# Holding TensorE's written order in one group, moving a background reduction, and scaling the feed-forward input in another place

## The chip, the cores and the metric

The kernel runs on one core of one Trainium2 chip. The metric is the device time of one execution in microseconds (us). The core has a matrix engine (TensorE, in the profile PE for products and PEld for weight loads), a vector engine (VectorE, DVE), a scalar engine (ScalarE, ACT), GpSimd (POOL), and SyncE (SP), which here issues transfers only. Each engine works through its own queue in order.

## The reference

One layer of a bidirectional encoder block in 32-bit floats, with 256 tokens of width 2048, followed by a final RMS norm:

```python
mod = silu(c) @ ada_w + ada_b            # 12288 values: shift, scale, gate, twice
h = rms_norm(x, norm_mix_w) * (1 + scale_m) + shift_m
proj = h @ w_in                          # inputs of both branches, gates
y_a = (sigmoid(a_o) * rms_norm(mlstm_fwd + mlstm_bwd)) @ w_branch_a     # 4 heads
y_b = (rms_norm(delta_fwd + delta_bwd) * silu(b_z)) @ w_branch_b        # 16 heads
x = x + gate_m * ((g_a * y_a + g_b * y_b) @ w_out)
hf = rms_norm(x, norm_ffn_w) * (1 + scale_f) + shift_f
gt, up = split(hf @ w_gate_up)
x = x + gate_f * ((silu(gt) * up) @ w_down)
return rms_norm(x, norm_final_w)
```

The delta rule (branch B) needs, for each head, direction and chunk, the inverse of a unit triangular matrix. The kernel inverts 32 x 32 blocks on VectorE and puts larger ones together with small matrix products.

## The kernel before

**Products.** Every large product is made in three passes: a weight tile is split into a high part (`wh`, ScalarE, line 171 or 197) and a low part (`wl`, VectorE, line 172 or 198), and TensorE sums high x high, high x low and low x high. Weights arrive in pieces of 1 MB in four `raw` buffers (issued by SyncE); `wh` and `wl` have three buffers each. A product of 512 columns is a `tjob` of 8 steps with 12 matmuls each (k0 of two kinds per piece); a product of 128 columns is an `fjob` of 2 steps with 24 narrower matmuls.

**Filling jobs.** Around the delta rule, such jobs wait in the list `fills`: `v`, `mb`, `o`, `a`, `ma` (inputs of the mLSTM branch and the merge gates; in the trace the names raw_v, acc_ma and so on) and `z`. `fill(n)` issues their next n steps between the stages of other work. After every second step of a `tjob`, and once an `fjob`, `pump()` counts, and every `every[0]`-th count issues one *sum*.

**Sums.** The modulation values of parts 2 to 5 are not made on TensorE. Sum b of a part loads 1 MB of `ada_w` (transposed) and multiplies and adds it on VectorE (line 127): 16 sums and one small addition a part. Parts 2, 3 and 4 go into the list `background` before the delta rule (line 874), part 5 behind the product with `w_out` (line 1172). Beside the pumps, the loop of that product issues sums at listed steps (line 1163), and at step 4 of its last quarter all that are left.

**The delta rule.** Four groups of four heads (line 891). Per group: `invert` (VectorE, 30 dependent pairs of small products, lines 663 and 669, between filling steps; its result is stored to memory), `gdn_blocks` (loads it back, transposes it, mixes it into `R`, lines 682 to 689, and copies it to `X` and `UL`), and then two pairs of heads, each with stages in which TensorE, VectorE and ScalarE alternate: p1 (line 717, reads `R`), p2, p3, p4 (lines 726 to 751), pa, pb, pc (lines 763 to 776), po (785 to 790), px (796). Between two stages come one to four steps of the next group's head jobs `b` or of filling jobs; the tuple `last` (line 864) sets how many in the last group. As written, in that group: the end of o2 and all of a2, p1 of the first pair, ma2, mb3, o3 and the start of a3 spread over the stages, and behind the last stage the rest of a3, ma3, the first mLSTM products (`psc`, line 957), the rest of ma3 and `yb` (the product with `w_branch_b`).

**Who orders the work.** The program is traced in the written order and then scheduled by a planner that simulates it: on each engine, the first-written instruction that is ready in the simulation goes next. So a filling step can be moved ahead of a stage that isn't ready. `order(...)` pins an instruction behind everything traced before it on its engine, with no wait for its end. Before the change, TensorE's instructions of the delta rule are not pinned.

**The feed-forward input.** The product with `w_out` runs in quarters o0 to o3; o3 ends token half by token half. For each half, `residual` (lines 1113 to 1115) and `token_rstd` give the norm's factor `rs1`. Then `normed` scales x by quarters into `xn` (two buffers), `moved` transposes two halves on TensorE (`pxn`, line 1200), applies scale and shift (line 1204 or 1206) and takes the high part, and `low` the low part. This is pinned, and interleaved with the steps of the first gate job `gt0`: step n of `gt0` uses blocks 2n and 2n+1.

Of the kernel before, what the change touches and what calls it, by code (L numbers as in the profile page):

```python
# [12 lines left out]
ALU = mybir.AluOpType  # L13
# [38 lines left out]
@with_exitstack  # L52
def hybrid_block(ctx: ExitStack, tc: tile.TileContext, xr, nfr, crow, pk_d, cst_d, ada2, ada4, win0, winb, wint, wba, wbb, wo, wgu, wd, out, dbg=None):
    nc = tc.nc
    V, S, G, PE = nc.vector, nc.scalar, nc.gpsimd, nc.tensor

    def pool(stack, name, bufs=1, **kw):
        return stack.enter_context(tc.tile_pool(name=name, bufs=bufs, **kw))
# [27 lines left out]
    def order(ins, yes=True):  # L86

        return tc.keep_in_program_order(ins) if yes else ins
# [46 lines left out]
    def row_store(part, rp, factor=1.0):  # L135

        pr = gps(f"row{part}")
        PE.transpose(pr[0:KB, 0:P], mod[:, part * KB : (part + 1) * KB], ident)
        sm = rp.tile([KB, P], F32, name=f"rowsm{part}")
        S.activation(sm, pr[0:KB, 0:P], AF.Copy, scale=factor)  # L140
        G.dma_start(row_d[part].rearrange("(b p) -> b p", b=KB), sm)
# [5 lines left out]
    count, every = [0], [0]  # L147

    def sums(n=1):

        while n and background:
            if next(background[0], None):
                n -= 1
            else:
                background.pop(0)
# [89 lines left out]
    def run(job):  # L245
        for _ in job:
            pass
# [3 lines left out]
    def fill(n=1):  # L251

        while n and fills:
            if next(fills[0], None):
                n -= 1
            else:
                fills.pop(0)
# [85 lines left out]
    def z_job(g, early=0):  # L343
        def done(ps):
            szs[g] = evp.tile([P, 2, 512], F32, tag="sz", bufs=1, name=f"sz{g}")
            for t in range(2):
                S.activation(szs[g][:, t], ps[t], AF.Silu)
        return tjob(f"z{g}", [wint[g, u] for u in range(4)], hh, hl, done, early)
# [329 lines left out]
    def gdn_blocks(g):  # L678

        cg = bk.tile([P, 2, 512], F32, tag="uu", bufs=1, name=f"cg{g}")  # L680
        for b in range(4):
            G.dma_start(cg[32 * b : 32 * b + 32, 0], inv_d[g][:, 16 * b : 16 * b + 16].rearrange("j m i -> j (m i)"))
        yield
        order(V.transpose(cg[:, 1], cg[:, 0]))
        F_, Bt, Ft, B_ = (cg[:, i // 2, (i % 2) * 256 : (i % 2 + 1) * 256].rearrange("p (m c) -> p m c", m=8) for i in range(4))

        def mix(dst, a, ca, b, cb):
            order(V.tensor_scalar(dst, b, cb, None, ALU.mult))
            order(V.scalar_tensor_tensor(dst, a, ca, dst, ALU.mult, ALU.add))

        mix(R[:, 0], Ft, even, Bt, odd)
        mix(R[:, 1], B_, even, F_, odd)
        yield
        for i, ab in enumerate(((Ft, Bt), (B_, F_))):
            for b in range(4):
                r = slice(32 * b, 32 * b + 32)
                order(S.activation(X[r, i, :, b % 2], ab[b // 2][r], AF.Copy))
            yield
        for i, a in enumerate((F_, B_)):
            for b in range(4):  # L700
                r = slice(32 * b, 32 * b + 32)
                order(S.activation(UL[r, i, :, r], a[r], AF.Copy))
            yield
# [132 lines left out]
    def stream(h0):  # L836

        todo = []

        def piece():  # L840

            for q in list(todo):
                q[0] -= 1
                if not q[0]:
                    todo.remove(q)
                    next(heads1[q[1]])

        for h in range(h0, min(h0 + 2, NH_B)):
            for j in range(3):
                for _ in b_job(h, j):  # L850
                    piece()
                    yield True
            todo += [[2, h], [4, h]]
        while todo:
            fill(1)
            piece()
            yield True
        while True:
            fill(1)
            yield True  # L860
# [16 lines left out]
    def invert(g):  # L877
        gen = gdn_invert(g)
        next(gen)
        fill(4)  # L880
        for _ in gen:
            fill(1)

    def o_load(g, where, bufs):
        o4 = where.tile([P, 4, T], F32, tag="o4", bufs=bufs, name=f"o4_{g}")
        G.dma_start(o4, ob_d[g].rearrange("h p t -> p h t"))
        return o4
# [3 lines left out]
    for g in range(4):  # L891
        if g == 3:
            sf.close()
            op = pool(so, "op", side="right")
        blocks = gdn_blocks(g)
        next(blocks)
        fill(8)
        next(blocks)
        fill(1)
        pairs = [gdn_phase2(g, p) for p in range(2)]  # L900
        every[0] = (0, 2, 2, 2)[g]
        for p in range(2):
            pieces = stream(4 * g + 2 * p + 4)
            if g == 3:
                o4s += [o_load(i, op, 3) for i in ((0, 1), (2,))[p]]
            for n in range(1, 10):
                next(pairs[p], None)
                if p == 0:
                    next(blocks, None)
                for _ in range(after[n] if g < 3 else last[n]):  # L910
                    next(pieces)
            for _ in pairs[p]:
                pass

            if g < 3:
                while 4 * g + 2 * p + 5 not in heads:
                    next(pieces)
        if g < 3:
            fills.insert(0, z_job(g + 1))
            every[0] = 0  # L920
            invert(g + 1)
# [146 lines left out]
    fill(4)  # L1068
    next(cores)
    fill(1000)  # L1070
    so.close()
    sa.close()
    sd = ExitStack()
# [14 lines left out]
    mgh, mgl = big(bigC, F32R, "mgh"), big(bigC, F32R, "mgl")  # L1088
    for g in range(4):
        if g == 3:  # L1090
            every[0] = 0
            while len(background) > 2:
                sums()
            row_store(2, ml, 0.5)
        run(y_a(g, mgh, mgl))
# [21 lines left out]
    def root():  # L1117

        order(S.activation(rs1[:, 2:3], ones1, AF.Sqrt))
# [8 lines left out]
    rs1 = xp.tile([P, 3], F32, name="rs1")  # L1128
# [23 lines left out]
    for g in range(4):  # L1152
        def done_o(*a, g=g):
            for t, ps in [a] if g == 3 else enumerate(a[0]):
                residual(t, g, ps, gm, ss1, wp, g == 3)
                if g == 3:
                    token_rstd(ss1, rs1, t)

        if g == 3:
            root()  # L1160
        between = (lambda: next(gt0)) if g == 3 else None
        for i, _ in enumerate(tjob(f"o{g}", [wo[g, u] for u in range(4)], mgh, mgl, done_o, by_token=between)):
            if i in ((4, 6, 7), (1, 2, 4, 6), (1, 2, 4, 6), (1, 2, 4))[g]:
                sums()
            if g == 3 and i == 4:
                sums(P)
                V.scalar_tensor_tensor(
                    affn, mod[:, 4 * KB : 5 * KB], 1.0, pk[:, PK_NFFN : PK_NFFN + KB], ALU.add, ALU.mult
                )
# [16 lines left out]
    def normed(q, t, parts, eng):  # L1186
        if q not in xns:
            xns[q] = hp.tile([P, 2, 512], F32, tag="sg", bufs=2, name=f"xn{q}")
        o, i = xns[q][:, t, parts], x1[:, t, q * 512 + parts.start : q * 512 + parts.stop]
        if eng is V:  # L1190
            order(V.tensor_scalar(o, i, rs1[:, t : t + 1], None, ALU.mult))
        else:
            order(S.activation(o, i, AF.Copy, scale=rs1[:, t : t + 1]))

    def moved(b):

        px = gps(f"pxn{b}")
        for t in range(2):
            f = b % 4 * P
            order(PE.transpose(px[:, t * P : (t + 1) * P], xns[b // 4][:, t, f : f + P], ident))  # L1200
        hfs[b] = hp.tile([P, T], F32, tag="hf", bufs=2, name=f"hf{b}")
        f, m = affn[:, b : b + 1], mod[:, 3 * KB + b : 3 * KB + b + 1]
        if b % 2 and b > 2:
            order(S.activation(hfs[b], px[:, 0:T], AF.Identity, scale=f, bias=m))
        else:
            order(V.tensor_scalar(hfs[b], px[:, 0:T], f, m, ALU.mult, ALU.add))
        order(S.activation(hfh[:, b], hfs[b], AF.Copy))
# [5 lines left out]
    normed(0, 1, slice(0, 256), V)  # L1213
    for t in range(2):
        normed(0, t, slice(256, 512), S)
    moved(0)
    moved(1)
    low(0)
# [4 lines left out]
    for b in range(2, KB, 2):  # L1223

        next(gt0)
        low(b)
        low(b + 1)
        next(gt0)
        if b % 4 == 2 and b < 12:
            for t in range(2):  # L1230
                normed(b // 4 + 1, t, slice(0, 512), S)
        for e in (b + 2, b + 3):
            if e < KB:
                moved(e)
# [3 lines left out]
    for j in range(FB // 4):  # L1238
# [4 lines left out]
        for e2 in range(2):  # L1243
# [5 lines left out]
            b = 4 * j + 2 * e2  # L1249
# [144 lines left out]
```

## Time and profile before

| | |
|---|---|
| median of 3 runs | 1985.31 us (1982.88 to 1988.02) |
| the profiled execution | 1979.27 us, span 1977.3 us, mean granted clock of TensorE 0.988 |
| TensorE busy | 1918.9 us, 97% of the span |
| VectorE, ScalarE, GpSimd busy | 71%, 52%, 5% |
| memory traffic | 246 GB/s on average |
| one sum on VectorE | 2.29 us, 64 of them |

The stages in the trace, from the span's start: first product up to 138 us; delta rule's groups from about 314, 482, 665 and 862 us (their first p1); `yb` from 952, `ya` from 1076, o0 to o3 from 1169 to 1254, feed-forward input from 1260 to 1292, gate and up products to 1738, down product to the end.

A row of waits names the waiting instruction and, behind the arrow, who released it. In a row of a group stand the line, engine, operation, output and inputs, shapes and count, then busy us, mean ns of one, and the idle time of the engine before it. Durations of one execution are compared with its own span; the runs' median is another number.

### The profile page before, as it was taken

The numbers are of one execution on the slowest core, as the hardware profiler recorded it, in microseconds if no ns is written. First come the engines' busy times: TensorE is split into PE (matmuls) and PEld (weight loads), VectorE is DVE, ScalarE is ACT, GpSimd is POOL, SyncE is SP. The second block draws the span as 40 slices with busy tenths as digits, with TensorE's granted clock in tenths as the row PEclk, the third lists the DMA queues.
The fourth block names the chain that finished last, engine by engine and source line by source line (L and its number), as shares of the span: only waits on it lengthen the run. The fifth ranks groups of instructions, "written<-read, shape, count | busy, mean of one in ns | idle before, by whom it ended". The sixth has DMA issues, their size and how long they took to land.

```text
span 1977.3 us, 27036 instructions
## 1 busy us (share of the span) xinstructions
PE 1918.9 (97%) x10352; PEld 1705.5 (86%) x10352; DVE 1402.5 (71%) x2091; ACT 1022.7 (52%) x1568; POOL 96.9 (5%) x185
## 2 busy tenths in 40 slices
PE   8999999999999999999799999799999999999997
PEld 6887889989989998998688888688888888888886
DVE  5779887878988996965587769766666655555554
ACT  3146657855765686465454444554444444444443
POOL 0000300110100011000200000000000000000000
PEclk9999999999999999999799999899999999999999
DMA  9996665567667765885677679466766765566563
GB/s 400 420 383 194 222 223 192 167 203 283 228 199 247 281 214 191 310 303 190 234 291 266 249 288 419 182 234 235 265 244 237 262 246 193 205 240 203 202 206 114
DMA packets 78675, 487.76 MB, mean 247 GB/s; under 512 B 10265, under 2 KB 15681, under 8 KB 23889
## 3 DMA queue, kind: packets, MB, share of 16 engines
q1 hardware_dynamic: 63360, 450.95, 62.2%
q0 software_dynamic: 7872, 19.99, 4.4%
q10 hardware_dynamic: 7314, 15.10, 2.1%
q8 instruction: 81, 1.33, 0.3%
q14 instruction: 48, 0.39, 0.1%
HBM read 469.16 MB, written 16.83 MB: 246 GB/s over the span
## 4 chain that ended last, share of the span: by engine, by line
PE 73%; DVE 11%; DMA 9%; ACT 4%; issue 2%; POOL 0%; SPq 0%; ACTq 0%; DVEq 0%; POOLq 0%
DMA ra<-ada 5%; PE acc_up L215 4%; PE acc_up L218 4%; PE acc_up L216 4%; PE acc_d L216 4%; PE acc_d L215 4%; PE acc_d L218 4%; PE acc_gt L216 4%; PE acc_gt L215 4%; PE acc_gt L218 4%; PE acc_o L218 2%; PE acc_o L216 2%; PE acc_o L215 2%; PE acc_a L175 2%; PE acc_b L175 2%
## 5 line engine op out<-in xcount | busy, mean ns | idle before, releaser
L198 DVE TENSOR_TENSOR wl_d<-raw_d,wh_d 128x1024 fp32r<-128x1024 f32 x88 | 107.8, 1225 | 102.7 <-ACT wh_d L197 102.7
L127 DVE SCALAR_TENSOR_TENSOR ada<-ada,crow 128x2048 f32<-128x2048 f32 x64 | 146.5, 2289 | 43.6 <-DMA ada<-ada 43.5
L198 DVE TENSOR_TENSOR wl_up<-raw_up,wh_up 128x1024 fp32r<-128x1024 f32 x88 | 107.5, 1225 | 95.9 <-ACT wh_up L197 95.9
L197 ACT ACTIVATE wh_d<-raw_d 128x1024 fp32r<-128x1024 f32 x88 | 93.0, 1057 | 130.5 <-PE acc_d L216 125.3
L198 DVE TENSOR_TENSOR wl_gt<-raw_gt,wh_gt 128x1024 fp32r<-128x1024 f32 x88 | 107.7, 1224 | 72.4 <-ACT wh_gt L197 68.2
L197 ACT ACTIVATE wh_gt<-raw_gt 128x1024 fp32r<-128x1024 f32 x88 | 92.9, 1056 | 120.7 <-PE acc_gt L216 73.2
L197 ACT ACTIVATE wh_up<-raw_up 128x1024 fp32r<-128x1024 f32 x88 | 93.0, 1056 | 118.2 <-PE acc_up L216 71.7
L215 PE MATMUL acc_gt<-wh_gt,hfh 128*128 128x512 f32 x352 | 135.2, 384 | 0.0
L216 PE MATMUL acc_gt<-wh_gt,hfl 128*128 128x512 f32 x352 | 134.6, 382 | 0.0
L175 PE MATMUL acc_b<-hh,wh_b 128*128 128x256 f32 x576 | 134.6, 276 | 0.0
L175 PE MATMUL acc_b<-hl,wh_b 128*128 128x256 f32 x576 | 134.6, 277 | 0.0
L215 PE MATMUL acc_up<-wh_up,hfh 128*128 128x512 f32 x352 | 133.5, 379 | 0.0
L216 PE MATMUL acc_up<-wh_up,hfl 128*128 128x512 f32 x352 | 133.5, 379 | 0.0
L216 PE MATMUL acc_d<-wh_d,ffl 128*128 128x512 f32 x344 | 130.4, 379 | 0.0
L215 PE MATMUL acc_d<-wh_d,ffh 128*128 128x512 f32 x344 | 130.4, 379 | 0.0
L530 PE MATMUL first<-x,raw 128*128 128x256 f32 x512 | 114.5, 382 | 7.5 <-ACT x L523 6.8
L530 PEld LDWEIGHTS first<-x,raw 128*128 128x128 f32 x512 | 96.1, 190 | 25.9 <-ACT x L523 12.4
L175 PEld LDWEIGHTS acc_b<-hl,wh_b 128*128 128x128 f32 x576 | 110.6, 192 | 0.4
L175 PEld LDWEIGHTS acc_b<-hh,wh_b 128*128 128x128 f32 x576 | 110.5, 192 | 0.5
L197 ACT ACTIVATE wh_o<-raw_o 128x1024 fp32r<-128x1024 f32 x64 | 67.1, 1054 | 58.9 <-PE acc_o L216 35.5
L218 PE MATMUL acc_gt<-wl_gt,hfh 128*128 128x512 f32 x352 | 95.3, 385 | 0.0
L171 ACT ACTIVATE wh_b<-raw_b 128x1024 fp32r<-128x1024 f32 x72 | 76.1, 1058 | 37.1 <-PE acc_b L175 22.8
(384 smaller groups left out, 5018.4 us busy)
## 6 DMA issues: line engine op xcount, KB each, us to landing
ada<-ada SPq DMA_DIRECT2D x64, 1024.0 KB, 5.8
raw_gt<-wgu SPq DMA_DIRECT2D x44, 1024.0 KB, 5.0
raw_up<-wgu SPq DMA_DIRECT2D x44, 1024.0 KB, 4.9
raw_d<-wd SPq DMA_DIRECT2D x44, 1024.0 KB, 4.9
raw_b<-winb SPq DMA_DIRECT2D x36, 1024.0 KB, 5.0
ra<-ada SPq DMA_DIRECT2D x32, 1025.0 KB, 15.8
raw<-win SPq DMA_DIRECT2D x16, 1024.0 KB, 17.1
raw_z<-wint SPq DMA_DIRECT2D x16, 1024.0 KB, 5.2
```

Source lines behind the costliest of these rows:

```text
L127: V.scalar_tensor_tensor(raw, raw, 1.0, row_c[:, :D], ALU.mult, ALU.mult, accum_out=mod[:, c0 + b : c0 + b + 1])
L171: S.activation(wh, raw[:, k0 : k0 + 8], AF.Copy)
L175: PE.matmul(o, wh[:, k], both(x, k0 + k).rearrange("p a b -> p b a"), start=k0 + k + i == 0, stop=False)
L197: order(S.activation(wh, raws[u][:, k0 : k0 + 2], AF.Copy), hold)
L198: order(V.tensor_tensor(wl, raws[u][:, k0 : k0 + 2], wh.bitcast(F32), ALU.subtract), hold)
L215: order(PE.matmul(ps[t], tok(xh, kk, t), turns(wh[:, k]), start=kk == 0, stop=False), early and steps > 1)
L216: PE.matmul(ps[t], tok(xl, kk, t), turns(wh[:, k]), start=False, stop=False)
L218: PE.matmul(ps[t], tok(xh, kk, t), turns(wl[:, k]), start=False, stop=kk == last)
L530: PE.matmul(first[o], raw[:, o], x[:, b], start=b == 0 and o % 2 == 0, stop=b == KB - 1 and o % 2 == 1)
```

## The change

TensorE's products and transposes go through a small class that pins them while `pin[0]` is true: from the start of the delta rule's last group to the end of the filling jobs. Group 0 of the delta rule issues a sum at every third count; `every[0] = 0` ahead of the last quarter of `ya` is gone, so it stays 2 until the feed-forward loop is over; the listed sums in o1 to o3 are fewer. `normed` can run on GpSimd, does so for quarter 1 early, and quarters 2 and 3 are scaled at blocks 4 and 8 and not at 6 and 10.

```diff
-    V, S, G, PE = nc.vector, nc.scalar, nc.gpsimd, nc.tensor
+    V, S, G = nc.vector, nc.scalar, nc.gpsimd
+    pin = [False]
+    class Tensor:
+        def matmul(self, *a, **k):
+            return order(nc.tensor.matmul(*a, **k), pin[0])
+        def transpose(self, *a, **k):
+            return order(nc.tensor.transpose(*a, **k), pin[0])
+    PE = Tensor()
...
         if g == 3:
             sf.close()
             op = pool(so, "op", side="right")
+            pin[0] = True
...
-        every[0] = (0, 2, 2, 2)[g]
+        every[0] = (3, 2, 2, 2)[g]
...
     fill(1000)
+    pin[0] = False
     so.close()
...
         if g == 3:
-            every[0] = 0
             while len(background) > 2:
                 sums()
...
-            if i in ((4, 6, 7), (1, 2, 4, 6), (1, 2, 4, 6), (1, 2, 4))[g]:
+            if i in ((4, 6, 7), (2, 4, 6), (1, 3), ())[g]:
                 sums()
...
-        if eng is V:
-            order(V.tensor_scalar(o, i, rs1[:, t : t + 1], None, ALU.mult))
+        if eng is not S:
+            order(eng.tensor_scalar(o, i, rs1[:, t : t + 1], None, ALU.mult))
...
+    for t in range(2):
+        normed(1, t, slice(0, 512), G)
     moved(0)
...
-        if b % 4 == 2 and b < 12:
+        if b % 4 == 0 and b < 12:
             for t in range(2):
                 normed(b // 4 + 1, t, slice(0, 512), S)
```

## The prediction

> **What bounds the kernel now.** I read the page first, then TensorE's waits, then stretches of the span, then single places. The profiled execution took 1979.27 us (span 1977.3 us, 2.0 us around it); the three runs have a median of 1985.31 us, 6.0 us above it. So I make the sum against 1979.27 us and add its difference to 1985.31 us. Repeated runs spread by 0.26%, so I take 0.3%, 6.0 us, as the least change that a measurement can tell from none.
>
> ```profile
> PE 1918.9 (97%) x10352; PEld 1705.5 (86%) x10352; DVE 1402.5 (71%) x2091; ACT 1022.7 (52%) x1568; POOL 96.9 (5%) x185
> ```
>
> TensorE sets the end; other engines count only where TensorE idles or its clock is low. TensorE's waits, over the whole span and then between 930 and 975 us, say where it idles (us in total, times, longest):
>
> ```profile
> PE pxn L1200 <- ACT xn L1193: 11.6, 7, 6.8
> ...
> PE psc L957 <- DMA mkq<-kq_d: 3.7, 2, 3.3
> PE acc_yb L215 <- ACT obh L932: 3.5, 1, 3.5
> PE px L796 <- DVE on L819: 3.3, 1, 3.3
> PE pb L775 <- DVE r L776: 2.3, 1, 2.3
> PE po L786 <- ACT z L768: 0.7, 1, 0.7
> ...
> PE pden L981 <- DVE mdec L966: 0.5, 1, 0.5
> ```
>
> Two places matter: the end of the delta rule's last group (3.7 + 3.5 + 3.3 + 2.3 + 0.7 + 0.6 + 0.5 = 14.6 us) and the feed-forward's input (11.6 us). Both also lower the clock. The stretches (length; busy us of PE, PEld, DVE, ACT, POOL; granted clock; DMA share; GB/s), and below them four short ones with PE alone:
>
> ```profile
> 336.00:420.00 84.00, 82.69 (x613) 78.63 (x614) 68.62 (x170) 64.71 (x142) 13.91 (x28) 1.00 0.55 159
> 817.00:861.50 44.50, 44.50 (x208) 38.99 (x207) 37.35 (x58) 20.68 (x25) 2.85 (x5) 1.00 0.85 312
> 930.00:982.00 52.00, 37.38 (x160) 30.70 (x159) 24.21 (x46) 23.50 (x43) 10.77 (x18) 0.77 0.60 212
> 1169.00:1253.00 84.00, 83.49 (x391) 72.91 (x390) 73.08 (x73) 36.87 (x46) 0.55 (x1) 1.00 0.98 400
> 945.90:956.30 10.40, 5.91 (x14) 0.51 0.47 158
> 966.40:980.20 13.80, 13.31 (x44) 0.51 0.47 158
> 1256.50:1263.50 7.00, 2.99 (x11) 0.51 0.00 0
> 1277.00:1280.50 3.50, 3.50 (x10) 0.51 0.00 0
> ```
>
> At half clock, half of the busy time is lost: (5.91 + 13.31) / 2 = 9.6 us at the group's end, 1.5 and 1.75 us at the feed-forward's input. So the group's end costs 14.6 + 9.6 = 24.2 us today, the feed-forward's input 11.6 + 3.25 = 14.9 us.
>
> **Part 1: TensorE's order held from the last group on.** The end is dry because the planner spent the filling jobs early. As written, the group's first product (p1, line 717) stands right behind job a2, and ma2, mb3 and the first sixth of o3 come only behind it. Where the trace has them:
>
> ```profile
> L177 PE MATMUL acc_a<-hh,wl_a x64: 275/275/276, 796.9 to 816.5; 128*128 128x256 f32 x64
> L717 PE MATMUL p<-R,cc x8: 192/276/276, 861.7 to 862.4; 128*128 128x32 f32 x8
> ```
>
> Held, TensorE comes to p1 at 816.8 us and not at 861.7 us; 44.9 us of fill (the 44.5 us full stretch above) stand queued behind it, and ScalarE and VectorE can split only three steps ahead. p1 reads R, the end of a chain: 60 small VectorE products of the inversion, a store, a load, a transpose, the mix. VectorE and its rows between 816 and 862 us, then the chain's end (start, length):
>
> ```profile
> L127 DVE SCALAR_TENSOR_TENSOR ada<-ada,crow 128x2048 f32<-128x2048 f32 x5 | 11.4, 2288 | 1.5 <-DMA ada<-ada 1.5
> L198 DVE TENSOR_TENSOR wl_mb<-raw_mb,wh_mb 128x1024 fp32r<-128x1024 f32 x8 | 9.7, 1217 | 1.4 <-ACT wh_mb L197 1.3
> L198 DVE TENSOR_TENSOR wl_ma<-raw_ma,wh_ma 128x1024 fp32r<-128x1024 f32 x6 | 7.3, 1214 | 0.2 <-ACT wh_ma L197 0.2
> L663 DVE TENSOR_TENSOR utmp<-uu 64x238 f32<-64x238 f32 (+13 forms) x14 | 4.4, 314 | 0.3
> L669 DVE TENSOR_TENSOR uu<-uu,utmp 64x238 f32<-64x238 f32 (+13 forms) x14 | 4.4, 313 | 0.2
> ```
> ```profile
> 844.05 0.17 DVE L669 TENSOR_TENSOR uu<-uu,utmp 64x30 f32<-64x30 f32 x1
> ...
> 857.03 0.71 DVE L684 STREAM_TRANSPOSE cg<-cg 128x512 f32<-128x512 f32 x1 [2.54 <-DMA cg<-inv_d]
> 857.67 0.31 DVE L688 TENSOR_SCALAR R<-cg,cst 128x256 f32<-128x256 f32 x1
> ...
> 859.03 0.48 DVE L689 SCALAR_TENSOR_TENSOR R<-cg,cst,R 128x256 f32<-128x256 f32 x1
> ```
>
> So R is far from ready at 816.8 us. But the chain will run faster: at that time 4.4 + 4.4 = 8.8 us of it are left, and what slows it today is the splitting of weights (9.7 + 7.3 us) and the modulation sums (11.4 us), which feed a TensorE that would now stand still. One more split and one sum remain: 816.8 + 8.8 + 1.2 + 2.3 = 829.1 us. Store and load took 857.03 - 844.22 = 12.8 us amid a DMA share of 0.85; I take 10.5, as the weight stream stops too (it keeps four raw buffers). Transpose and first mix: 0.71 + 0.31 + 0.48 = 1.5 us. R at 841 us: **a wait of 24 us**, bounded by 19 (only the 8.8 us and a 9 us transfer) and 43 (R at 859.5 us as now). Then some 4 us at half clock, as behind the stalls above: +2.0 us.
>
> What it buys. The waits that have to be covered, and how long psc was in coming:
>
> ```profile
> 946.25 0.73 PE L796 MATMUL px<-cst,on 128*128 128x128 f32 x2 [3.34 <-DVE on L819]
> 947.54 0.69 PE L796 MATMUL px<-cst,on 128*128 128x128 f32 x2 [0.56 <-ACT obt L798]
> ...
> 965.24 2.62 PE L957 MATMUL psc<-mkq 128*128 128x256 f32 x8 [3.33 <-DMA mkq<-kq_d]
> ```
>
> As written, behind every stage of the group stand one to three steps of a filling job (the full stretch above: 44.5 us / 208 = 0.214 us a matmul, 12 in a step, 2.6 us). Behind its last stage come 6 steps of a3 (24 narrow matmuls; the 192 of a2 in the first fence of this part took 21 us, so 2.7 us each), 4 of ma3, psc, 4 more of ma3, yb: 27 us before psc and 37 us before yb, where psc's data came 17 us behind px. I expect 3.5 us of the 24.2 to stay (z and r are waited for one step later): -20.7 us. Bounds: 0 and -24.2. **Part 1: +24 + 2 - 20.7 = +5.3 us.**
>
> **Part 2: the sums.** Counting the pumps of the filling jobs: group 0 has 16 (numbers 27 to 42), so every third gives 6 sums, where it had none. Groups 1 to 3, yb and ya0 to ya2 keep their 8, 8, 7, 8 and 6; ya3 gets 2. All 48 sums of three parts are then done by the first step of o1, where today 13 fall between 1169 and 1261 us:
>
> ```profile
> L127 DVE SCALAR_TENSOR_TENSOR ada<-ada,crow 128x2048 f32<-128x2048 f32 x13 | 29.7, 2287 | 2.6 <-DMA ada<-ada 2.6
> ```
>
> Cost: 6 x 2.29 = 13.7 us of VectorE put where it is busy 68.62 of 84 us. TensorE has fills there to run ahead with, so it will hardly stall at once; but the chain to R starts later, and what had been absorbed by more fill is, with part 1, added to the wait at p1. Bounds 0 and +13.7; I take **+4 us**, nearer to nothing, since VectorE had 15 us of idle time there. In o itself TensorE was busy 83.49 of 84 us, so the empty VectorE gains nothing before the last quarter's end.
>
> There it does (start, length):
>
> ```profile
> 1251.16 0.69 DVE L1113 TENSOR_TENSOR tmss<-acc_o,gm 128x512 f32<-128x512 f32 x1 [1.14 <-PE acc_o L241]
> 1251.77 2.28 DVE L127 SCALAR_TENSOR_TENSOR ada<-ada,crow 128x2048 f32<-128x2048 f32 x1
> ...
> 1256.05 0.67 DVE L1113 TENSOR_TENSOR tmss<-acc_o,gm 128x512 f32<-128x512 f32 x1
> ...
> 1257.37 2.28 DVE L127 SCALAR_TENSOR_TENSOR ada<-ada,crow 128x2048 f32<-128x2048 f32 x1
> ...
> 1258.02 0.19 ACT L1115 ACTIVATION_READ_ACCUMULATOR tmss<-x 128x1 f32 x1
> ...
> 1260.51 1.97 PE L1200 MATMUL pxn<-cst,xn 128*128 128x128 f32 x8 [6.79 <-ACT xn L1193]
> ```
>
> TensorE was done at 1260.51 - 6.79 = 1253.72 us. Without the two sums the second half's tm starts at 1253.75, 2.3 us sooner, and its reduce follows the square (1258.21) and not the sum (1259.65), 1.2 us more when the reads are counted: -3.5 us. But line 1091 also goes: every stays 2 until the loop of the feed-forward input is over, so two of gt0's four pumps (numbers 178 and 180) now put a sum of part 5 and its 1 MB load into that loop (the first takes a raw buffer ahead of gt0's last piece, on SyncE's queue). VectorE's held instructions behind the first (low(8)) queue behind it, and the planner can put it into the very gap that the old sums leave: +1 us (0 to +2.3).
>
> **Part 3: the scaling.** Today ScalarE scales a quarter directly ahead of its transposes; a row of the second such stop:
>
> ```profile
> 1275.75 0.33 PE L1200 MATMUL pxn<-cst,xn 128*128 128x128 f32 x1 [1.72 <-ACT xn L1193]
> ```
>
> The later stops together are 11.6 - 6.8 = 4.8 us, and the 1.75 us at half clock from 1277 us follow from this one. Quarter 1 goes to GpSimd, quarters 2 and 3 one turn (two blocks) ahead of use, and the buffers are free by then. GpSimd has no such row; its nearest is a memset of that shape, the ScalarE row is the same work:
>
> ```profile
> L552 POOL MEMSET cc<- 128x512 f32 x6 | 2.9, 521 | 5.7 <-DMA raw_v<-wint 5.7
> L1193 ACT ACTIVATE xn<-x,rs 128x512 f32<-128x512 f32 x6 | 4.0, 706 | 0.0
> ```
>
> Between 0.5 and, four times that, 2.1 us each (an estimate; I take 1.0, near the ScalarE row). The eight transposes and twelve matmuls ahead of quarter 1's give some 4.6 us, so even two of 2.1 us are hidden. I take 0.5 us of the stops as left: -4.3 - 1.75 = -6.0 us (bounds -2 and -6.6). **Parts 2 and 3: +4 - 3.5 + 1 - 6.0 = -4.5 us.**
>
> The wait ahead of the first transposes shrinks to 6.79 - 3.5 = 3.3 us. The 3.34 us stall before px lowered the clock, and the stop of 1.72 us did too, so I leave the 1.5 us of half clock there. The Trainium skill ("TensorE: Matmul & The Clock Gate", Part 1) has the clock halved only after an idle window of about 3.4 us; by it the clock would hold and the sum be 1.5 us lower. These rows speak against that.
>
> **Sum:** +5.3 - 4.5 = +0.8 us: 1980 us of the profiled kind, 1986 us as a median.
>
> **Rivals.** (a) *The wait at p1 is short, faster.* For: 11.4 + 9.7 + 7.3 = 28.4 of VectorE's 37.35 us between 817 and 861.5 us are sums and splits. Against: 12.8 us of transfers don't shrink with VectorE. With a wait of 10 us: 14 us less, 1972 us. (b) *The wait at p1 is as long as today's lead, slower.* The inversion keeps its pace, because the six sums of group 0 reach it late and other VectorE work stays planned between its steps; R comes at 860 us, the wait is 43 us: +19 us, 2005 us. It decides from a wait of 30 us on. For: 60 dependent steps and two transfers, all unhidden then. Against: the splits are held back by three buffers. (c) *The held order changes nothing*, as the planner's had been this one: then -4.5, and 3 of the sums' 4 us absorbed too, 1978 us. Against: p1 stands 44.9 us behind its written place.
>
> **Chances.** Forecast (within 6 us) 0.37; (a) 0.27; (b) 0.30; (c) 0.06. So faster 0.33, same 0.37, slower 0.30. Around the likeliest 1980 to 1992; the range reaches well into (a) and just short of all of (b): 1968 to 2004.
>
> **What would show it.** A TensorE wait of 20 us or more for R at line 717, no more waits at pb, px, yb and psc, clock 1.00 between 930 and 980 us; xn waits down to one of some 3.5 us; six sums between 310 and 420 us. The forecast is wrong if line 717 waits under 15 or over 30 us, or if the group's end stays dry.

## The result, and the profile after

The changed kernel takes 2055.42 us (median of 4 runs, 2049.6 to 2062.11), beside 1986.66 us for the kernel before in the same session: a ratio of 1.0349 (95% interval 1.0312 to 1.0387), 69 us slower. The forecast was 1986 us, with a range of 1968 to 2004. The profiled execution took 2049.6 us (span 2047.6). That of before (1979.27 us) lies some 7 us below its median, so spans of single executions differ by a little more than medians do; below, times are compared by ratios of runs, and the traces tell where they went.

From the page of the kernel after: TensorE's line, and TensorE and its granted clock in 40 slices of 51 us.

```profile
PE 1932.9 (94%) x10352; PEld 1712.3 (84%) x10352; DVE 1401.6 (68%) x2091; ACT 1027.5 (50%) x1569; POOL 100.5 (5%) x187
...
PE   8999999999998999459999999989999999999998
...
PEclk9999999999998999679999999999999999999999
```

TensorE does the same 10352 instructions and is 14 us busier, by lower clock; the rest of the 70 us of span is idle time. Most of both lies in the delta rule's end: from group 2's first product to `yb` TensorE idles 63 us (761 to 1031 us), in the kernel before 12 us (665 to 952 us). Waits of TensorE from 800 to 1050 us (us in total, times, longest; the matmuls now carry the line of the new class, so the tiles tell them apart), and stretches around the longest (length; busy us of PE, PEld, DVE, ACT, POOL; clock; DMA share; GB/s):

```profile
PE p L62 <- ACT X L709: 38.9, 1, 38.9
PE p L62 <- DVE pt L730: 5.5, 1, 5.5
PE pb L62 <- DVE r L788: 5.0, 2, 2.6
PE acc_ma L62 <- ACT wh_ma L209: 3.9, 1, 3.9
```
```profile
820.00:848.00 28.00, 20.75 (x100) 18.17 (x100) 13.75 (x52) 12.44 (x42) 3.94 (x8) 0.68 0.18 65
848.50:887.50 39.00, 0.48 (x3) 0.51 (x3) 23.03 (x73) 4.48 (x15) 8.65 (x14) 0.50 0.22 62
...
892.00:980.00 88.00, 81.26 (x445) 72.49 (x445) 45.97 (x56) 50.26 (x98) 0.00 (x0) 0.98 0.62 218
```

TensorE stands 38.9 us before the last group's first product, and the 28 us ahead of it are thin as well (20.75 us busy, at a clock of 0.68: the end of group 2's second pair, without fill between its stages). The old dry end is no longer dry: 81.26 of 88 us at a clock of 0.98.

What went wrong began far earlier. VectorE during the inversion ahead of group 1, from its first to its last instruction, in the kernel before (424.6 to 464.5 us: 40 us) and after (456.9 to 550.7 us: 94 us); columns: line, engine, operation, tiles and shapes, count, then busy us, mean ns of one, idle time before:

```profile
L198 DVE TENSOR_TENSOR wl_mb<-raw_mb,wh_mb 128x1024 fp32r<-128x1024 f32 x8 | 9.7, 1209 | 0.0
L663 DVE TENSOR_TENSOR utmp<-uu 64x58 f32<-64x58 f32 (+14 forms) x29 | 9.5, 326 | 0.8
L669 DVE TENSOR_TENSOR uu<-uu,utmp 64x58 f32<-64x58 f32 (+14 forms) x29 | 9.4, 325 | 0.7
L198 DVE TENSOR_TENSOR wl_ma<-raw_ma,wh_ma 128x1024 fp32r<-128x1024 f32 x4 | 4.8, 1210 | 0.0
L172 DVE TENSOR_TENSOR wl_b<-raw_b,wh_b 128x1024 fp32r<-128x1024 f32 x3 | 3.6, 1213 | 0.1
```
```profile
L184 DVE TENSOR_TENSOR wl_b<-raw_b,wh_b 128x1024 fp32r<-128x1024 f32 x24 | 29.0, 1210 | 0.2 <-ACT wh_b L183 0.2
L330 DVE SCALAR_TENSOR_TENSOR cv<-pad,pk,cv 128x256 f32<-128x256 f32 x40 | 18.2, 469 | 0.0
L139 DVE SCALAR_TENSOR_TENSOR ada<-ada,crow 128x2048 f32<-128x2048 f32 x8 | 18.2, 2280 | 1.9 <-DMA ada<-ada 1.9
...
L681 DVE TENSOR_TENSOR uu<-uu,utmp 64x30 f32<-64x30 f32 (+14 forms) x30 | 9.5, 318 | 0.4
L675 DVE TENSOR_TENSOR utmp<-uu 64x30 f32<-64x30 f32 (+14 forms) x30 | 9.5, 317 | 0.3
```

The inversion's own work is 19 us in both. In the kernel before it shares VectorE with the splits of filling jobs (`wl_mb`, `wl_ma`). In the kernel after the inversion starts 32 us later, but these filling jobs do not: `mb` runs from 440 to 464 us, in the kernel before from 438 to 459 us, so its splits are over when the inversion starts. TensorE works mostly on the next group's head jobs then: 24 splits, 40 convolution steps and 8 sums of group 1, 65 us, stand between the inversion's steps, beside 11 splits of filling jobs (`o`, `a`, `z`), 13 us. A head job brings VectorE two splits, four convolution steps and, every second time, a sum: 2 x 1.21 + 4 x 0.47 + 1.14 = 5.4 us, against the 5.4 us that TensorE takes for its two steps (2.7 us each, from the prediction's row of a2). By this estimate it fills VectorE by itself, while a filling step brings 1.21 us of split per 2.6 us. In the trace VectorE is busy 90.47 of the 93.5 us from 457 to 550.5 us, and TensorE all of them.

The feed-forward's input after: TensorE's waits, then rows of VectorE (start, length) and of GpSimd.

```profile
PE pxn L65 <- ACT xn L1206: 6.2, 1, 6.2
PE acc_gt L62 <- ACT hfh L1220: 4.0, 4, 2.7
```
```profile
1324.63 2.29 DVE L139 SCALAR_TENSOR_TENSOR ada<-ada,crow 128x2048 f32<-128x2048 f32 x1 [0.53 <-DMA ada<-ada]
...
1326.85 0.69 DVE L1127 TENSOR_TENSOR x<-x,tmss 128x512 f32<-128x512 f32 x1
...
1342.44 2.29 DVE L139 SCALAR_TENSOR_TENSOR ada<-ada,crow 128x2048 f32<-128x2048 f32 x1 [0.70 <-DMA ada<-ada]
```
```profile
1329.18 1.57 POOL L1204 TENSOR_SCALAR xn<-x,rs 128x512 f32<-128x512 f32 x1 [82.90 <-DVE rs L1138]
1331.97 1.73 POOL L1204 TENSOR_SCALAR xn<-x,rs 128x512 f32<-128x512 f32 x1 [1.22 <-DVE rs L1138]
```

The later `xn` stops are gone. The first sum of part 5 stands exactly in the gap that the old sums left, between the last product with the gate and the addition to x; the second delays `low` in the loop (the 2.7 us stop).

### The profile page after: what moved, and what is told of

The parts are those of the page before. It is cut to its first block, busy times and chain, and to the rows that moved or that the text cites. A ratio compares the mean times of both kernels' runs of the same rounds, so it can differ in the third digit from the quotient of the medians.

```text
span 2047.6 us, 27053 instructions
## 1 busy us (share of the span) xinstructions
PE 1932.9 (94%) x10352; PEld 1712.3 (84%) x10352; DVE 1401.6 (68%) x2091; ACT 1027.5 (50%) x1569; POOL 100.5 (5%) x187
## 5 line engine op out<-in xcount | busy, mean ns | idle before, releaser
L183 ACT ACTIVATE wh_b<-raw_b 128x1024 fp32r<-128x1024 f32 x72 | 76.2, 1060 | 64.5 <-PE acc_b L62 37.1
L210 DVE TENSOR_TENSOR wl_o<-raw_o,wh_o 128x1024 fp32r<-128x1024 f32 x64 | 77.2, 1219 | 31.8 <-ACT wh_o L209 31.5
```

Of the source, the lines that this page charges most:

```text
L183: S.activation(wh, raw[:, k0 : k0 + 8], AF.Copy)
L210: order(V.tensor_tensor(wl, raws[u][:, k0 : k0 + 2], wh.bitcast(F32), ALU.subtract), hold)
```

## The experiments

Differences in us are (ratio - 1) x the median of before in the same session (1983 to 1987 us).

### The change taken apart

`pin_alone` has only the hold, `group0_sums_alone` only `every[0]` of 3 in group 0, `scaling_alone` only the sooner scaling; `no_pin` is the change without the hold:

```diff
-            pin[0] = True
```

> The kernel before with TensorE's order held from the last group's start to the end of the filling jobs, and nothing else. Theory A (the hold and the six sums of group 0 cost so much only together: the sums let the filling jobs be spent early and make R late, the hold then forbids what is left to run): the wait at p1 is about the 24 us of the prediction's first part, the group's dry end is gone, and the time is 0 to 12 us above before. Theory B (the hold alone is the cause): 45 to 75 us above before, with a wait of 35 us or more at p1. Theory C (the sums of group 0 alone): within 6 us of before.

> The changed kernel without the hold (sums and scaling stay). Theory A: the late R is then partly covered by ma2, mb3 and o3, so 10 to 35 us above before. Theory B: 3 to 10 us below before. Theory C: 50 to 75 us above before, as much as the change itself.

> The kernel before with one edit: every third count of group 0 issues a sum (six sums more there, six fewer later). Theory A: 15 to 35 us above before, and the last group's first p1 at least 20 us later than the 862 us of before. Theory B: within 6 us. Theory C: 50 us or more above before.

> The kernel before with the third part alone: quarter 1 scaled on GpSimd early, quarters 2 and 3 at blocks 4 and 8. All theories: the stops of 1.5, 1.7 and 0.7 us ahead of the later transposes go, and with them the half clock after the second; 4 to 7 us below before if nothing takes their place, within 2 us of before if the steps of the first gate job become bound by VectorE or ScalarE instead (the changed kernel shows four waits for hfh, one of them 2.7 us beside a sum of part 5, three of 0.4 us without one).

| | ratio to before (95%) | us |
|---|---|---|
| hold alone | 1.0058 (1.0038 to 1.0078) | +11.5 |
| change without hold | 1.0306 (1.0274 to 1.0337) | +60.8 |
| group 0's sums alone | 1.0282 (1.0262 to 1.0302) | +56.0 |
| scaling alone | 0.9969 (0.9954 to 0.9983) | -6.2 |

The six sums are the fault, without the hold as with it. I had held a cost that only both together bring (theory A) for possible; it is refuted. Theory C, the sums alone, has all but one reading: it put the hold alone within 6 us of before, and that cost 11.5 us. In the run with these sums alone the inversion ahead of group 1 again takes 94 us (458.8 to 552.6), that ahead of group 2 takes 75 us, and the first products of groups 1, 2 and 3 come at 570, 763 and 956 us, where they came at 483, 665 and 862. TensorE stays busy meanwhile (it idles 11 us from 338 to 763 us); the bill comes where no fill is left. Stretches of before, then of this run:

```profile
800.00:955.00 155.00, 144.54 (x901) 131.82 (x901) 101.72 (x144) 81.85 (x140) 7.32 (x12) 0.97 0.72 256
955.00:1060.00 105.00, 100.84 (x456) 87.31 (x455) 78.66 (x115) 48.81 (x65) 8.75 (x16) 0.91 0.76 280
```
```profile
800.00:955.00 155.00, 139.13 (x821) 125.17 (x819) 113.77 (x221) 85.39 (x146) 17.25 (x31) 0.96 0.74 259
955.00:1060.00 105.00, 77.87 (x309) 66.39 (x310) 39.77 (x75) 42.75 (x100) 11.84 (x20) 0.64 0.33 109
```

Between 955 and 1060 us TensorE idles for 27 us and works the other 78 at a mean clock of 0.64: the last group's stages follow each other with no filling job between them (the last one, `ma`, ends at 946 us).

### Work, loads or order

The six sums in group 0 again, with VectorE's work on them taken away and their loads kept, so this version leaves these six values out (theory O is the order on VectorE, W the work, L the loads):

```diff
+            n = 2 if part == 2 and b < 6 else D
-            V.scalar_tensor_tensor(raw, raw, 1.0, row_c[:, :D], ALU.mult, ALU.mult, accum_out=mod[:, c0 + b : c0 + b + 1])
+            V.scalar_tensor_tensor(raw[:, :n], raw[:, :n], 1.0, row_c[:, :n], ALU.mult, ALU.mult, accum_out=mod[:, c0 + b : c0 + b + 1])
```

> The kernel before with the six sums in group 0, of which VectorE multiplies 2 columns in place of 2048 (the loads and the raw buffers stay; the sums of part 2's first six rows are left out, some 13.7 us of VectorE). Theory O (order): the cost of +56 us comes from where the planner puts the head jobs' splits and convolutions on VectorE, in between the steps of the inversions, since the inversion then starts after the next heads' jobs are already ready; it takes little to tip that, so this stays slower than before by 25 to 60 us, with the inversion of group 1 or 2 longer than 70 us. Theory W (work): the 13.7 us of VectorE in a stretch where it is full are multiplied along the chain; with the work gone the time is within 6 us of before and each inversion lasts about 40 us. Theory L (loads): the loads hold raw buffers and delay the weights behind them; also +25 or more, but with inversions of 40 us and TensorE waiting for wh.

Ratio 1.0171 (1.0155 to 1.0188), +33.9 us: without 13.7 us of VectorE work three fifths of the loss remain. The inversions ahead of groups 1 and 2 take 69 and 86 us, and in the second (636 to 722 us) VectorE does the work of the next head jobs again:

```profile
L173 DVE TENSOR_TENSOR wl_b<-raw_b,wh_b 128x1024 fp32r<-128x1024 f32 x23 | 27.8, 1210 | 0.0
L319 DVE SCALAR_TENSOR_TENSOR cv<-pad,pk,cv 128x256 f32<-128x256 f32 x40 | 18.3, 470 | 0.0
```

So W falls as the whole cause; the 22 us that went with the work may be its own price or a better order, which this run does not tell apart. L, which asked for inversions of 40 us, falls as the loads' direct cost; that the loads are what sets the inversion back (it starts at 438 and not 425 us) stands.

Then the head jobs' splits were kept behind the inversions, first all of them:

```diff
-            V.tensor_tensor(wl, raw[:, k0 : k0 + 8], wh.bitcast(F32), ALU.subtract)
+            order(V.tensor_tensor(wl, raw[:, k0 : k0 + 8], wh.bitcast(F32), ALU.subtract), name[0] == "b")
```

> The kernel before with the six sums in group 0 in full, and the low-part splits of the head jobs (b jobs, line 172) kept in program order on VectorE, so that none can stand between the steps of an inversion written ahead of it. Theory O: inversions back at about 40 us, cost against its control (the held splits alone) 5 to 16 us, the six sums' own 13.7 us of VectorE or less. Theory W: still 40 us or more above the control. Theory L: as W, with inversions of 40 us.

> The control: the kernel before with only the head jobs' splits kept in program order. All theories: 0 to +15 us (a held split can make TensorE wait for it in the groups' pairs, where products of the pairs and head jobs alternate), inversions about 40 us.

The control alone cost 1.0523 (1.0500 to 1.0546), +104 us and not the 0 to 15 expected: held splits make TensorE wait, 22 us at the groups' first products and 15 us in 8 waits at `vps` among others. With the six sums it is 1.0469 (1.0447 to 1.0491). The sums cost nothing there (it is even faster with them), and inversions take 34 to 42 us, but a kernel with this much idle time is a poor witness. So only the first split behind two inversions was held, with the mixes of `gdn_blocks` unpinned so that the split need not wait for them:

```diff
-            V.tensor_tensor(wl, raw[:, k0 : k0 + 8], wh.bitcast(F32), ALU.subtract)
+            order(V.tensor_tensor(wl, raw[:, k0 : k0 + 8], wh.bitcast(F32), ALU.subtract), name in ("b8_0", "b12_0") and k0 == 0)
...
-        order(V.transpose(cg[:, 1], cg[:, 0]))
+        V.transpose(cg[:, 1], cg[:, 0])
...
-            order(V.tensor_scalar(dst, b, cb, None, ALU.mult))
-            order(V.scalar_tensor_tensor(dst, a, ca, dst, ALU.mult, ALU.add))
+            V.tensor_scalar(dst, b, cb, None, ALU.mult)
+            V.scalar_tensor_tensor(dst, a, ca, dst, ALU.mult, ALU.add)
```

> The kernel before with the six sums in group 0, and of the head jobs' splits only the first one behind the inversions of groups 1 and 2 (b8_0 and b12_0, one instruction each) kept behind the inversion on VectorE; the mixes behind the inversion are left free. Theory O (the late inversion shares VectorE with the head jobs): the inversion of group 1 takes 20 to 30 us in place of 94 and that of group 2 about 40, the first product of group 1 comes at 505 to 525 us in place of 570, TensorE waits there 10 to 25 us as the fill work is used up, and the cost against its control is 10 to 30 us, in place of 56. Theory W (the sums' 13.7 us of VectorE or their loads do it wherever the head jobs stand): the cost against the control stays at 45 us or more.

> The control: the kernel before with only these two splits held and the mixes free. All theories: 0 to +25 us (the head jobs start up to 19 us later than the 464 us of before, some of it without other work for TensorE); inversions of 30 to 40 us.

Control 1.0129 (1.0099 to 1.0158), with the sums 1.0218 (1.0183 to 1.0252): the six sums cost 43.2 - 25.6 = 17.6 us (some 9 to 26), not 56. The inversion ahead of group 1 takes 26 us (459.1 to 485.1), and this time VectorE does little beside it:

```profile
L669 DVE TENSOR_TENSOR uu<-uu,utmp 64x30 f32<-64x30 f32 (+14 forms) x30 | 9.7, 323 | 1.0
L663 DVE TENSOR_TENSOR utmp<-uu 64x30 f32<-64x30 f32 (+14 forms) x30 | 9.7, 322 | 1.0
L198 DVE TENSOR_TENSOR wl_o<-raw_o,wh_o 128x1024 fp32r<-128x1024 f32 x2 | 2.5, 1226 | 0.2 <-ACT wh_o L197 0.2
L127 DVE SCALAR_TENSOR_TENSOR ada<-ada,crow 128x2048 f32<-128x2048 f32 x1 | 2.3, 2285 | 0.0
```

It starts 34 us late all the same, as in `group0_sums_alone`, and TensorE waits 20.1 us at group 1's first product, where it waits 12.0 us in the control and not at all in the kernel before (waits from 455 to 700 us):

```profile
PE p L717 <- DVE R L689: 25.0, 2, 20.1
```

So about two thirds of the 56 us hang on what stands between the inversion's steps. The share is rough, since part of the sums' cost can hide in the control's own 25.6 us of loss.

### Number or place

Three sums (every sixth job), three sums in the second pair alone, and six sums under the inversion itself:

```diff
-        every[0] = (0, 2, 2, 2)[g]
+        every[0] = (6, 2, 2, 2)[g]
```
```diff
             pieces = stream(4 * g + 2 * p + 4)
+            if g == 0:
+                every[0] = 3 * p
```
```diff
-        for _ in gen:
+        for i, _ in enumerate(gen):
             fill(1)
+            if g == 1 and i < 6:
+                sums()
```

> The kernel before with a sum at every sixth head job of group 0 in place of every third: three sums, not six. By number and work: half of 56, 25 to 31 us. By the falling behind (an inversion shares VectorE with head jobs or it does not): 35 to 56 us, with the inversion of group 1 or 2 at 70 us or more.

> The kernel before with sums in group 0 at every third job of its second pair alone (two or three sums). By number and work: 18 to 28 us, the inversion of group 1 the longest. By the falling behind: the inversion of group 1 stays at 40 to 45 us and that of group 2, further on, is the one that goes over 70 us; cost 20 to 45 us.

> The kernel before with six sums written behind the first six pauses of group 2's predecessor, the inversion of group 1, and none in group 0. By number and work: 40 to 60 us, since they meet an inversion directly. By the falling behind: the inversion of group 1 grows by no more than the 13.7 us of the sums' own work, that of group 2 goes over 60 us, cost 20 to 45 us.

| | ratio (95%) | us | inversion 0, 1, 2, 3 (us) |
|---|---|---|---|
| before | 1 | 0 | 38, 40, 41, 50 |
| loads alone | 1.0171 (1.0155 to 1.0188) | +33.9 | 40, 69, 86, 43 |
| six sums | 1.0282 (1.0262 to 1.0302) | +56.0 | 56, 94, 75, 42 |
| three sums | 1.0288 (1.0257 to 1.0318) | +57.1 | 42, 79, 78, 40 |
| three, second pair | 1.0125 (1.0099 to 1.0152) | +24.8 | 38, 44, 87, 44 |
| six under inversion 1 | 1.0217 (1.0186 to 1.0249) | +43.0 | 38, 55, 75, 48 |

Three sums cost as much as six, and three that stand later cost less than half. In the last two rows the inversion next to the sums grows by 4 and 15 us, and it is the following one that about doubles. A price by the number or the work of the sums is out. What fits every row: once an inversion comes late, the fill meant for it has run before it, and it comes under head jobs; the earlier that begins, the more inversions it takes. This is read from the traces: no run changed the amount of fill alone. (Five of the six sums of the last row ran ahead of the inversion, from 404 us on, and the sixth under its first steps, since VectorE was free to take them; that they'd meet it directly was my mistake.)

### The hold

In `pin_alone`: the inversion's last step, the load's end with the transpose and the last mix on VectorE, and TensorE's stretches:

```profile
828.48 0.18 DVE L679 TENSOR_TENSOR uu<-uu,utmp 64x30 f32<-64x30 f32 x1
836.28 0.71 DVE L694 STREAM_TRANSPOSE cg<-cg 128x512 f32<-128x512 f32 x1 [7.63 <-DMA cg<-inv_d]
...
838.05 0.48 DVE L699 SCALAR_TENSOR_TENSOR R<-cg,cst,R 128x256 f32<-128x256 f32 x1
```
```profile
818.00:838.00 20.00, 0.19 (x1) 0.20 (x2) 11.44 (x33) 0.93 (x3) 2.85 (x5) 0.57 0.32 118
838.00:842.00 4.00, 4.00 (x14) 3.55 (x15) 1.19 (x3) 0.72 (x2) 0.00 (x0) 0.50 0.00 0
842.00:846.00 4.00, 4.00 (x18) 3.38 (x17) 0.96 (x1) 1.06 (x1) 0.00 (x0) 0.66 0.00 0
...
850.00:871.00 21.00, 17.41 (x94) 15.23 (x93) 14.22 (x14) 13.40 (x24) 0.00 (x0) 1.00 0.54 177
...
930.00:982.00 52.00, 47.35 (x318) 43.72 (x317) 28.64 (x41) 27.40 (x40) 10.27 (x17) 0.97 0.80 287
```

TensorE waits 20.9 us (24 forecast), and the old dry end, 37.38 of 52 us at 0.77 before, is now 47.35 at 0.97. But the pairs between pay for it, with waits of 6.6 us in all at pb and 3.7 us at acc_ma for its split (3.6 us of them from 850 to 871 us). These two traces are 23 us apart from group 2's first product to `ya` (434 and 411 us), twice the 11.5 us of the runs: the profiled execution of `pin_alone` is the slowest of its seven, and that of before is below its median. So the traces show where the hold costs, and the runs how much.

Two versions without group 0's sums, with the scaling, the spread o sums and the pump stopped behind o: one with the hold, one with the hold from the second pair of the last group on, so that nothing is held at the first product. Both have the first edit below, the second version also the other one:

```diff
     background.append(ada_part(5, row_c))
+    every[0] = 0
...
             pieces = stream(4 * g + 2 * p + 4)
             if g == 3:
+                pin[0] = p == 1
```

> The hold, the sooner scaling and the o sums spread with the pump stopped, and no sums in group 0: the change without its main fault. If the hold costs the same +11.6 us here as alone: 1989 to 1992 us. If it takes its price only from the waits at the tail that this variant no longer has: 1978 to 1983 us.

> The run with scaling, o sums and stopped pump (1978.7), and the hold from the second pair of the last group on, its first pair left free. If the hold's price is the wait at the group's first product (20.9 us and some 10 us at the lower clock behind it) and its gain the dry end of 900 to 1000 us: no wait there, the excess of 900 to 1000 us down from 29 to 10 to 18 us, 1966 to 1973 us. If the dry end only moves with the fills: 1978 to 1985 us.

They take 1.0068 (1.0045 to 1.0091) and 1.0066 (1.0042 to 1.0090), where the same version without a hold takes 0.9974 (0.9964 to 0.9984): the hold costs 18.7 and 18 us, each known to some 5 us. In the second one the wait at the first product is 8.3 us and not 20, and the end from 900 us on is full, yet the loss has moved to the first pair:

```profile
848.00:870.00 22.00, 10.38 (x47) 9.10 (x46) 11.13 (x14) 6.52 (x14) 2.55 (x5) 0.71 0.70 245
...
900.00:1000.00 100.00, 93.93 (x562) 85.09 (x562) 57.91 (x75) 53.36 (x82) 10.85 (x18) 0.98 0.73 265
```

Fill held back for the end is missing where the planner used it, and the dry time moves with it; both forecasts of 1966 to 1973 us and of 5 us for the hold were built on its going away. But moving alone would have cost nothing: 1978 to 1985 us was forecast for that, and the run took 1998. From group 2's first product to `ya` it takes 434 us (665 to 1099) with TensorE busy for 402.35, where the version without a hold takes 417 us (665 to 1082) with 394.64 busy: 9 us more idle time and, as the work is the same, 8 us more at the lower clock. Why the dry time grows as it moves was not isolated.

### The o sums, part 5's sums, and a version meant to be faster

> The kernel before with the sooner scaling, the sums spread away from o's last quarter as in the change, no sums in group 0, no hold, and the pump stopped behind the o products so that no sum of part 5 falls into the feed-forward input. If the sums' spreading is worth what was predicted (-3.5 at o's end, the +1 of the two part-5 sums avoided): 1977 us, 8 to 11 us below before. If the spreading itself costs (the change without hold came out some 11 us dearer than the group-0 sums and the scaling together): 1985 to 1995 us.

> As the run with the sooner scaling and the o sums spread, but the pump not stopped, as in the change: two sums of part 5 come before and in the feed-forward input. By the prediction's +1 us for these two: 1979 to 1981 us beside 1978.7. If they cost what the change without the hold had beyond its parts (about 11 us): 1988 to 1992 us.

With the spread o sums and the pump stopped: 0.9974 (0.9964 to 0.9984), -5.2 us. From 8 to 11 us below before were expected. The first `pxn` wait falls from 6.9 us (scaling alone) to 3.5 us, as forecast (rows of the two traces below), yet the time is that of the scaling alone.

```profile
PE pxn L1200 <- ACT xn L1193: 6.9, 1, 6.9
```
```profile
PE pxn L1200 <- ACT xn L1193: 3.5, 1, 3.5
```

The traces show where the gain went. With `every[0] = 0` gone ahead of `ya`'s last quarter, six sums in place of three fall into `ya`, and TensorE waits there (rows of the version with the pump stopped; in the scaling alone these two waits are 0.5 and 1.0 us):

```profile
PE acc_ya L218 <- DVE wl_ya L198: 2.2, 3, 1.2
PE acc_ya L216 <- DVE hal L1024: 1.8, 1, 1.8
```

Lengths of three stretches in the traces (us), each from the first product of one kind to the first of the next:

| | `ya` | o to the first `pxn` | first `pxn` to the up product |
|---|---|---|---|
| before | 92.8 | 91.5 | 31.1 |
| scaling alone | 93.6 | 91.6 | 27.3 |
| and o sums spread, pump stopped | 97.6 | 88.1 | 27.3 |
| and o sums spread, pump left on | 97.9 | 88.1 | 31.3 |

So the spread sums gain 3.5 us at o's end and lose 4.0 us in `ya`.

With the pump left on: 1.0007 (0.9988 to 1.0026), 6.5 us more, where I had put 1. Two sums of part 5 then stand at the feed-forward's input, with new stops of 1.6 and 1.5 us in the loop, and that stretch is 4.0 us longer; the 6.5 us of the runs are known to some 4 us. Together with group 0's sums alone this version adds up to 56.0 + 1.4 = 57.4 us, beside 60.8 us for the change without the hold, so no large term is left over.

Last, the rule read the other way: three sums stand between the steps of the last inversion in the kernel before. Without them, with a sum at every count in `ya` in place of every second, and with the sooner scaling and the stopped pump as above:

```diff
             pieces = stream(4 * g + 2 * p + 4)
+            if g == 3:
+                every[0] = 2 * p
...
     for g in range(4):
+        every[0] = 1
         if g == 3:
-            every[0] = 0
```

> The kernel before with the sooner scaling, no sums in the first pair of the last group (three of these stand between the steps of its inversion, 794 to 844 us), a sum at every count in ya, so that all 48 are made ahead of o2, and the pump stopped behind o. No hold, no sums in group 0. If a lighter inversion brings the group forward: inversion 38 to 43 us in place of 50, first product at 845 to 855 us in place of 862, the wait ahead of the feed-forward's first transposes down by some 3.5 us, 1964 to 1974 us. If the time of the dry end is set by the amount of fill and not by when R comes: 1975 to 1979 us, from scaling and o alone. If the doubled sums in ya cost there (its memory traffic): over 1980 us, with waits for wl or wh at ya.

Ratio 1.0011 (0.9998 to 1.0023), no gain, and 8 us more than the scaling alone, which it contains. The inversion did go from 50 to 40 us and the first product came at 848 in place of 862 us, but `ya`, with 13 sums in it, took 101.6 us in place of 93.6, and o waited too:

```profile
PE acc_ya L216 <- DVE hal L1026: 4.2, 1, 4.2
PE acc_o L215 <- ACT wh_o L197: 3.7, 2, 3.0
```

No version was clearly faster than the scaling alone, 0.9969 of before.

## Why the prediction was wrong

**Part 2, the step that failed:** "Cost: 6 x 2.29 = 13.7 us of VectorE put where it is busy 68.62 of 84 us. TensorE has fills there to run ahead with, so it will hardly stall at once ... Bounds 0 and +13.7; I take +4 us". TensorE indeed did not stall at once. But the sums' own work was no upper bound, and "what had been absorbed by more fill" was named and not priced. Measured: +56.0 us, against 0 to +13.7, and more than the whole range had room for. I took the planner's order elsewhere as given. It isn't: the fill had run when the next inversion came, head jobs stood there in its stead, and with them the inversion took 94 us in place of 40 (75 in place of 41 the next time). In the run with these sums alone three of the six also landed under the first inversion (284 to 315 us) and not, as forecast, from 310 us on; it took 56 us in place of 38.

What is not isolated: how 13.7 us of work and six loads set the inversion ahead of group 1 back by 34 us (18 of these are the first inversion's longer time; with the loads alone it is 13 us).

**Part 1.** *The wait:* right. The inversion ended at 828.7 us (829.1 forecast), store and load took 7.6 us (10.5 taken, 9 the lower bound), R came at 838, the wait was 20.9 us (24 taken, 19 to 43). *The half clock behind it:* 6.9 us long, 3.5 us lost, not 4 and 2.0. *What it buys:* this term was mis-sized. I let 20.7 of 24.2 us come back as gain because the waits at the end could be covered; the fill that covers them was needed in the pairs before. By the 11.5 us of the runs, some 13 us came back (an estimate: 20.9 + 3.5 - 11.5). The hold costs 11.5 us alone, 18.7 us in the version above, and some 8 us within the change (1.0349 against 1.0306), not 5.3 (the intervals of the last two ratios overlap, so that 8 us is rough). The rival (b), a wait of 43 us since "the six sums of group 0 reach it late", is nearest to what the whole change shows: 38.9 us; but the inversion itself took only 21 us then, nothing stood between its steps, and it had started 62 us late.

**Parts 2 and 3, the feed-forward's input.** *The scaling:* the stops went as forecast and GpSimd's work was hidden (1.57 and 1.73 us; 1.0 taken, 0.5 to 2.1). The runs have -6.2 us (-9.1 to -3.4) for -6.0, but the trace shows 3.8 us at this place: three stops of 0.4 us came in at acc_gt, and the granted clock from 1250 to 1300 us is 0.90 in both traces, so the 1.75 us of half clock were not gained there. That the two numbers meet so closely is in part luck. *o's end:* right, 3.5 us, when no sum takes the gap; in the change the sum of part 5 took it, as the prediction feared, and the wait was 6.2 us where 3.3 were forecast. *The +1 for part 5's sums:* 4.0 us by the stretches, above its bound of 2.3. *A term that was missing:* "ya3 gets 2" was counted and not priced; the sums there cost 4.0 us, as much as o's end gained.

**What would show it.** Line 717's wait was over 30 us, which the prediction named as its refutation. In the last group the waits at yb and psc went, those at pb (5.0 us) and px (1.6 us) did not. The clock from 892 to 980 us was 0.98.

## What to carry to other kernels

Work put on an engine in a stretch where it has idle time is not priced by its own duration when a planner fills waits from a limited stock of independent jobs: ask what each delay spends of the stock, what stands in its place at the next long dependent chain, and how much of that chain's engine the substitute takes. Here a stall at the end of such a region came from a shortage of fill, and holding fill back moved the stall and did not remove it. A test of a price by the work is the dose: three units cost what six did.

## What the runs showed of the hardware

Behind the stop of 20.9 us TensorE ran at half clock for 6.9 us, behind that of 38.9 us for 4.8 us. The records of its matmuls tell it: eight products with R take 1.92 us there and 0.97 us behind it, one of 512 columns 0.63 us there and 0.38 us behind it. The granted clock agrees: 0.50 from 838 to 842 us and 0.66 from 842 to 846 us in `pin_alone`. From the traces of `pin_alone` and of the kernel after:

```profile
837.81 1.92 PE L60 MATMUL p<-R,cc 128*128 128x32 f32 x8 [20.94 <-DVE R L699]
...
844.76 0.97 PE L60 MATMUL p<-R,pt 128*128 128x32 f32 x8
```
```profile
887.02 1.89 PE L62 MATMUL p<-R,cc 128*128 128x32 f32 x8 [38.85 <-ACT X L709]
...
890.14 0.63 PE L62 MATMUL acc_ma<-wh_ma,hl 128*128 128x512 f32 x1
...
891.82 0.38 PE L62 MATMUL acc_ma<-wh_ma,hl 128*128 128x512 f32 x1
```

The Trainium skill ("TensorE: Matmul & The Clock Gate", Part 1) has the full clock back after at least one busy window of about 3.4 us of sustained work; here it took 4.8 and 6.9 us, so a sum that reckons with 3.4 us alone is too low by up to 1.8 us a stop (an estimate: half of 6.9 - 3.4).
